# Storing a mixer's split weights one use later, another order of places for them, and one state update moved by a unit

## The chip, the cores and the metric

The kernel runs on one core of one Trainium2 chip. The metric is the time of one execution on the device, in microseconds (us); a comparison uses the median of several executions. A core has five engines that run at the same time and meet through semaphores: TensorE (PE in the profile; PEld is its weight load), VectorE (DVE), ScalarE (ACT), GpSimd (POOL) and SyncE (SP), which here only issues DMA transfers. DMA transfers are also issued by ScalarE. Each engine takes its instructions in order.

## The reference

The reference is one step of a decoder layer, for a prompt of 2048 tokens with 16 meta tokens ahead of it, and for 8 samples of 4 tokens with their own states. All is float32, with a model width of 1024.

```
h = rmsnorm(x, norm_mix)
proj = h @ w_in                                  # 1024 -> 2568
lru_x, lru_gate, z, xbc, dt = split(proj)        # 512, 512, 512, 1024, 8
lru_out = rmsnorm(rg_lru(conv(lru_x)) * gelu(lru_gate))
xs, B, C = silu(conv(xbc))
y, state = ssd_chunked(xs, softplus(dt + bias), A, B, C, state)   # chunks of 128 tokens
ssd_out = rmsnorm((y + xs * d) * silu(z))
x = x + concat(lru_out, ssd_out) @ w_out
h = rmsnorm(x, norm_ffn)
g, v = conv(h @ w_up)                            # 1024 -> 2 * 3072
y = rmsnorm(x + (gelu(g) * v) @ w_down, norm_final)
```

`conv` is a short causal convolution over the tokens, `rg_lru` a gated linear recurrence. In `ssd_chunked` each chunk of 128 tokens gives an output within the chunk, an output from the state that came in, and an update of the state: `state = state * decay + B^T (decayed x dt)`. The next chunk's second output needs that state.

## The kernel before

**Precision.** TensorE multiplies in a rounded float32 (float32r). To keep float32's accuracy every operand is split into a high part, `hi = round(x)`, and a low part, `lo = x - hi`, and a product is three matmuls: hi*hi, hi*lo and lo*hi. A raw weight tile of 128 x 1024 (0.5 MB) is loaded by SP into a buffer `wraw`, of which there are two. ScalarE writes `whi` and VectorE `wlo` (lines 109 and 110, `divide`; the first tile's `wlo` is GpSimd's). The pair `whi`/`wlo` has three buffers each, called place `w` below.

**Stages.** Phase A is the mixer, in six row groups (`PLAN_A`): the samples and meta tokens with two prompt tiles (304 columns), four groups of three tiles of 128 tokens (384 columns) and one of two (256 columns). I call them stages 0 to 5. A stage has a main list, written out in `phase_a_tile`. With the dt product among them, it has 20 input projections, each with one weight tile of `w_in`: eight `xbc` tiles, four `lru`, four gate and four `z`. Then come the output projections: for two halves of the columns, two parts (lru and ssd) and each row tile, a unit of twelve matmuls. Each half and part uses two tiles of `w_out`, so eight tiles per stage; these are loaded raw and split in every stage.

Between the main units stand side tasks, in places written by hand (`SLOTS`): the decays (`R`, `decays`, `seg`), a chunk's work in three steps (`chunk2`, `chunk3`, `chunk4`), the recurrence's gates and scan, and the normalising (`norm`) and transposing (`turn`) of the next stage's rows. Stage 0 uses the list `first`, stages 1 to 3 `mid`, stage 4 `mid2`, and stage 5 `last`. `chunk41` is step 4 of the second row tile: two products give the state's update (line 741, into the psum tag `yy`), VectorE adds it to the state `S` (line 742), TensorE transposes `yt` (line 745, tag `tr`) and VectorE adds it to `ys` (line 747). `yt` comes from step 3 (line 728). Each psum tag has two banks. `chunk22` is step 2 of the third row tile: it transposes `xbc` into two banks of `tr` (lines 655, 658 and 660), from which VectorE and ScalarE make that chunk's operands (lines 662 to 668).

**Kept weights.** The 20 tiles of `w_in` are needed in all six stages. Class `Kept` (from line 129) keeps their split parts in DRAM, `khi` and `klo`. At the first use, in stage 0, the tile is loaded raw, split and used, and both parts are stored from its `whi`/`wlo` on ScalarE's DMA queue; `store` (line 160) issues a tile's two stores when the next tile is split. At each later use both parts are loaded by SP (line 151), 1 MB together, with no split. The place of a loaded pair comes from a cycle over five letters:

```
rooms = itertools.cycle("wwwxr")
```

`w` is a pair `whi`/`wlo`, `x` a fourth pair `xhi`/`xlo` in the pool `pa`, and `r` are the two raw buffers `wraw`, which then hold a high and a low part. So five pairs take turns, and since a stage has 20 tiles, a tile has the same place in each stage: positions 4, 9, 14 and 19 are `r`.

**Order.** TensorE's instructions run in the order of the program. For the other engines, from the end of the first norms until the last few units, a planner sets each engine's order at build time: it takes instructions as they become ready in its own timing model, the earlier in the program first. In the loop at the end of `build`, a source is loaded up to two units ahead of its use, four for `Kept`, and split up to two units ahead. A loaded `Kept` tile may only be issued once all raw tiles ahead of it are split.

Phase B, the channel mixer, follows from line 937 on. It uses `wraw`, `whi` and `wlo` in its own way and no `Kept` tile of the mixer.

Of the kernel before, what the change touches and what calls it, by code (L numbers as in the profile page):

```python
# [8 lines left out]
F32 = mybir.dt.float32  # L9
F32R = mybir.dt.float32r  # L10
# [7 lines left out]
P = 128  # L18
# [28 lines left out]
    },  # L47
    "mid": {
# [4 lines left out]
    },  # L53
# [20 lines left out]
def build(tc, i, o):  # L74
# [5 lines left out]
    with contextlib.ExitStack() as es:  # L80
        es.enter_context(tc.manual_schedule(engines={mybir.EngineType.PE}))
        cp = es.enter_context(tc.tile_pool(name="const", bufs=1))
        wp = es.enter_context(tc.tile_pool(name="w", bufs=3))
        pp = es.enter_context(tc.tile_pool(name="ps", bufs=2, space=PSUM))
        hp = es.enter_context(tc.tile_pool(name="h", bufs=1))
        dp = es.enter_context(tc.tile_pool(name="scr", bufs=1, space=DRAM))
        xr = es.enter_context(tc.tile_pool(name="xr", bufs=1, side="right"))
        side = es.enter_context(contextlib.ExitStack())
        pa = side.enter_context(tc.tile_pool(name="pa", bufs=1, side="right"))
# [18 lines left out]
        def divide(hi, lo, raw, E=V):  # L108
            A.activation(hi, raw, AF.Copy)  # L109
            E.tensor_tensor(lo, raw, hi.bitcast(F32), op=SUB)  # L110

        class Plain:
# [5 lines left out]
            def load(self):  # L118
                self.raw = self.room()
                ld(self.raw, self.src)  # L120

            def split(self, E=V):
                hi, lo = (wp.tile([P, 1024], F32R, name=nm, tag=nm) for nm in ("whi", "wlo"))
                divide(hi, lo, self.raw, E)
                self.out = hi, lo, self.raw

        kept, late = {}, []

        class Kept:

            rooms = itertools.cycle("wwwxr")

            def __init__(self, key, src):
                self.key, self.plain = key, Plain(src)
                self.ahead = KEPT_AHEAD

            def load(self):
                if self.key not in kept:
                    kept[self.key] = [dp.tile([P, 1024], F32, name=f"{nm}_{self.key}", tag=f"{nm}_{self.key}")
                                      for nm in ("khi", "klo")]  # L140
                    self.plain.load()
                    return
                room = next(self.rooms)
                if room == "w":
                    parts = [wp.tile([P, 1024], F32R, name=nm, tag=nm) for nm in ("whi", "wlo")]
                elif room == "x":
                    parts = [pa.tile([P, 1024], F32R, name=nm, tag=nm) for nm in ("xhi", "xlo")]
                else:
                    parts = [wp.tile([P, 1024], F32, name="wraw", tag="wraw", bufs=2).bitcast(F32R) for z in range(2)]
                for part, src in zip(parts, kept[self.key]):  # L150
                    ld(part.bitcast(F32), src)
                self.out = (*parts, None)

            def split(self, E=V):
                self.plain.split(E)
                self.out = self.plain.out
                store()
                late.extend((z, part.bitcast(F32)) for z, part in zip(kept[self.key], self.out))

        def store():  # L160

            for dst, src in late:
                A.dma_start(dst, src)
            late.clear()
# [80 lines left out]
        class Halves:  # L245
# [8 lines left out]
            def norm(self, q):  # L254
                rows, load = self.tiles[q]
                x = self.x[q] = k.spare_row() if q == 3 else row_tile()
                y = load(x)
                r = rstd_of(sum_squares(y[:rows], rows, D), rows, D)
                V.scalar_tensor_tensor(x[:rows], y[:rows], r[:rows], gain[:rows], op0=MUL, op1=MUL)
# [71 lines left out]

        flat = [s if hasattr(s, "load") else Plain(s) for fn, srcs in prog for s in srcs]
        loaded, split, used = 0, 0, 0
        early = sum(len(srcs) for _, srcs in prog[:k.begin_b]) + 2
        begin = contextlib.ExitStack()
# [1113 lines left out]
```

## Time and profile before

| | |
|---|---|
| median of 3 runs | 2574.25 us (2573.41 to 2576.53) |
| profiled execution | 2577.11 us, span of its instructions 2575.2 us |
| TensorE busy, share of span | 2461.2 us, 96% |
| VectorE, ScalarE, GpSimd busy | 1828.7, 1123.5, 665.8 us |
| mean granted TensorE clock | 0.982 |
| DMA | 559.80 MB, mean 217 GB/s |
| phase A | to about 956 us of the span |

In a row of the groups or the time line, `wlo<-wraw,whi` names what is written and read, L110 the line of the kernel, and the number in square brackets the idle time of the engine before the instruction and what ended it. A row of the waits has the waiting instruction, what it waited for, the total in us, how often, and the longest. The granted clock is the share of TensorE's full speed that it was given. SPq and ACTq are the queues that issue DMAs, and a DMA's last number is the time from issue to landing. Busy shares of engines that are not the bound say little by themselves: where TensorE is the bound, its idle time and what ended it count.

### The profile page before, as it was taken

The page shows a single profiled execution, that of the slowest core. Times are in us where ns is not written, and L with a number is a line of the kernel's source. Part 1 is how long each engine was busy: PE and PEld are TensorE (multiplying, and loading weights), DVE is VectorE, ACT ScalarE, POOL GpSimd, SP SyncE. Part 2 cuts the span into 40 slices and gives each one's busy share as a digit, 9 for nine tenths or more (in the row PEclk, how much of TensorE's full clock was granted, in tenths as well). Part 3 has the DMA queues.
Part 4 walks back from the last instruction along what each step waited for, and adds up shares of the span by engine and source line. Part 5 has one row for each costly group of instructions (what it writes and reads, how often), then busy time and mean ns, then how long its engine had stood idle before and what let it go on. Part 6 is the DMA issues. An engine that isn't in the chain of part 4 may idle for free.

```text
span 2575.2 us, 42314 instructions
## 1 busy us (share of the span) xinstructions
PE 2461.2 (96%) x15834; PEld 2233.6 (87%) x15834; DVE 1828.7 (71%) x2928; ACT 1123.5 (44%) x1905; POOL 665.8 (26%) x1059
## 2 busy tenths in 40 slices
PE   7889999998999998999998999999999999999998
PEld 6678879798897878988897899998999998999997
DVE  6675767667675767767767777777877777876776
ACT  4443534435353445444545443434443434433333
POOL 3432313223131326544555201101201102100001
PEclk9899999999999999999999999999999999999999
DMA  8657375473744767544646776665876665866663
GB/s 328 216 188 265 111 249 194 137 259 111 263 171 164 271 198 258 201 180 180 222 172 251 269 255 228 226 224 208 296 249 224 221 217 189 306 221 213 213 222 124
DMA packets 173959, 559.80 MB, mean 217 GB/s; under 512 B 25574, under 2 KB 25958, under 8 KB 173756
## 3 DMA queue, kind: packets, MB, share of 16 engines
q1 hardware_dynamic: 163284, 527.60, 58.2%
q10 hardware_dynamic: 10472, 29.50, 3.0%
q8 instruction: 125, 2.05, 0.3%
q14 instruction: 78, 0.64, 0.1%
HBM read 465.70 MB, written 91.34 MB: 216 GB/s over the span
## 4 chain that ended last, share of the span: by engine, by line
PE 66%; DVE 9%; issue 8%; POOL 7%; DMA 5%; ACT 5%; SPq 0%; POOLq 0%; ACTq 0%; DVEq 0%
PE mm L168 28%; PE sg L1172 14%; PE tr L168 9%; PE yy L168 9%; DVE wlo L110 2%; POOL wraw L1014 1%; ACT ws L109 1%; ACT whi L109 1%; POOL wraw L1013 1%; POOL o_fc L1157 1%; DVE cv L545 1%; POOL x L1015 1%; DMA wraw<-in_w_up 1%; DMA wk<-ws 1%; DVE xi L790 1%
## 5 line engine op out<-in xcount | busy, mean ns | idle before, releaser
L1172 PE MATMUL sg<-whi,ph 128*128 128x512 f32 x1320 | 424.1, 394 | 5.5 <-DVE acc L1176 5.5
L110 DVE TENSOR_TENSOR wlo<-wraw,whi 128x1024 fp32r<-128x1024 f32 x258 | 321.6, 1248 | 130.2 <-ACT whi L109 127.5
L109 ACT ACTIVATE whi<-wraw 128x1024 fp32r<-128x1024 f32 x259 | 272.9, 1056 | 243.2 <-PE sg L1172 90.1
L168 PE MATMUL mm<-hhi,whi 128*128 128x384 f32 (+4 forms) x1024 | 326.5, 319 | 7.7 <-ACT xr L536 6.5
L168 PE MATMUL mm<-hlo,whi 128*128 128x384 f32 (+4 forms) x1024 | 320.0, 312 | 0.9 <-DVE hlo L243 0.9
L168 PE MATMUL mm<-hhi,wlo 128*128 128x384 f32 (+4 forms) x1024 | 319.8, 312 | 1.1 <-DMA wlo<-klo 1.1
L1161 DVE SCALAR_TENSOR_TENSOR c<-u,fcw,c 128x512 f32<-128x512 f32 (+1 forms) x384 | 298.3, 791 | 23.7 <-ACT c L1159 14.1
L1172 PEld LDWEIGHTS sg<-whi,ph 128*128 128x128 f32 x1320 | 247.9, 188 | 65.0 <-DVE acc L1176 7.7
L1157 POOL COPY o_fc<-u 128x2 f32<-128x2 f32 x192 | 85.4, 445 | 807.2 <-DVE u L1066 696.3
L1172 PE MATMUL sg<-wlo,ph 128*128 128x512 f32 x660 | 258.6, 392 | 0.3 <-DVE wlo L110 0.3
L168 PEld LDWEIGHTS mm<-hhi,whi 128*128 128x128 f32 x1024 | 197.7, 193 | 12.7 <-ACT xr L536 7.0
L1159 ACT ACTIVATE c<-u,fcb,fcw 128x512 f32<-128x512 f32 (+1 forms) x192 | 157.8, 823 | 111.6 <-DVE u L1066 109.0
L168 PEld LDWEIGHTS mm<-hlo,whi 128*128 128x128 f32 x1024 | 197.3, 193 | 2.9 <-DVE hlo L243 1.2
L168 PEld LDWEIGHTS mm<-hhi,wlo 128*128 128x128 f32 x1024 | 197.1, 193 | 1.5 <-DMA wlo<-klo 1.5
L168 PE MATMUL yy<-h,ws 128*128 128x256 f32 x1476 | 196.4, 283 | 0.0
L168 PE MATMUL tr<-h,ws 128*128 128x256 f32 x1440 | 191.3, 282 | 2.0 <-DMA ws<-wk 2.0
L168 PEld LDWEIGHTS yy<-h,ws 128*128 128x128 f32 x1476 | 185.8, 189 | 1.0
L168 PE MATMUL mm<-h,ws 128*128 128x256 f32 x1404 | 185.8, 282 | 0.0
L545 DVE SCALAR_TENSOR_TENSOR cv<-xr,packed,cv 128x384 f32<-128x384 f32 (+2 forms) x216 | 150.6, 697 | 47.3 <-ACT cv L543 43.9
L168 PEld LDWEIGHTS tr<-h,ws 128*128 128x128 f32 x1440 | 180.5, 189 | 2.9 <-issue 2.2
L168 PEld LDWEIGHTS mm<-h,ws 128*128 128x128 f32 x1404 | 175.4, 188 | 0.5
L1172 PEld LDWEIGHTS sg<-wlo,ph 128*128 128x128 f32 x660 | 124.1, 188 | 25.2 <-DVE wlo L110 1.1
(321 smaller groups left out, 5377.5 us busy)
## 6 DMA issues: line engine op xcount, KB each, us to landing
ws<-wk SPq DMA_DIRECT2D x288, 512.0 KB, 4.9
wraw<-in_w_up SPq DMA_DIRECT2D x97, 512.0 KB, 4.9
wk<-ws SPq DMA_DIRECT2D x96, 512.0 KB, 6.4
wraw<-in_w_down SPq DMA_DIRECT2D x94, 512.0 KB, 4.9
wlo<-klo SPq DMA_DIRECT2D x60, 512.0 KB, 5.0
whi<-khi SPq DMA_DIRECT2D x60, 512.0 KB, 3.3
wraw<-in_w_out SPq DMA_DIRECT2D x48, 512.0 KB, 3.7
wraw<-in_w_up SPq DMA_DIRECT2D x72, 256.0 KB, 5.1
```

Of the source, the lines that this page charges most:

```text
L109: A.activation(hi, raw, AF.Copy)
L110: E.tensor_tensor(lo, raw, hi.bitcast(F32), op=SUB)
L168: PE.matmul(ps, l, r, start=(k == 0), stop=(k == len(pairs) - 1))
L545: V.scalar_tensor_tensor(cv[:, 3:W], buf[:, t:t + NC], w[:, t:t + 1], cv[:, 3:W], op0=MUL, op1=ADD)
L790: V.tensor_tensor_scan(h[:, 3:W], a4[:, j, 3:W], m4[:, j, 3:W], hc[:, j:j + 1], op0=MUL, op1=ADD)
L1013: G.tensor_tensor(v1, v0, v1, op=ADD)
L1014: G.tensor_tensor(v0, g0, v0, op=SUB)
L1015: G.tensor_tensor(g0, v1, g0, op=SUB)
L1157: G.tensor_copy(o_fc[:, g, NS, :], u[:, W - 2:W])
L1159: A.activation(cv[:, 2:W], u[:, 2:W], AF.Identity, scale=fcw[:, g, 2:3], bias=c["fcb"][:, g:g + 1])
L1161: V.scalar_tensor_tensor(cv[:, 2:W], u[:, z:z + W - 2], fcw[:, g, z:z + 1], cv[:, 2:W], op0=MUL, op1=ADD)
L1172: PE.matmul(ps, l, r, start=first and n == 0, stop=last and n == len(seq) - 1)
```

## The change

Three things change; what is computed stays the same.

1. A `Kept` tile counts its uses. Stage 0 loads it raw, splits it and stores nothing. Stage 1 loads it raw again and splits it again, now into one of four pairs in the order `wwwx`, and stores both parts (on ScalarE's queue, issued when the next tile is split). Stages 2 to 5 load the parts, as stages 1 to 5 did before. So 20 of 100 loads of pairs become raw loads with a split, and the stores move from stage 0 to stage 1.
2. The places of loaded parts follow `rwwxw`: positions 0, 5, 10 and 15 of a stage are `r`, the last one is `w`.
3. In stages 1 to 3 `chunk41` stands after the next main unit (the last gate projection), directly ahead of `chunk22`.

```diff
     "mid": {
-        12: "chunk40 R2 gates2", 13: "gates3 scan chunk21", 14: "chunk31 lru0", 15: "seg2 norm0 chunk41 lru1",
-        16: "chunk22 norm1 lru2", 17: "lru3 chunk32", 18: "chunk42 ssd0 rstd0 norm2", 19: "ssd1", 20: "ssd2",
+        12: "chunk40 R2 gates2", 13: "gates3 scan chunk21", 14: "chunk31 lru0", 15: "seg2 norm0 lru1",
+        16: "chunk41 chunk22 norm1 lru2", 17: "lru3 chunk32", 18: "chunk42 ssd0 rstd0 norm2", 19: "ssd1", 20: "ssd2",
...
         class Kept:
 
-            rooms = itertools.cycle("wwwxr")
+            rooms = itertools.cycle("rwwxw")
+            spare = itertools.cycle("wwwx")
+            uses = {}
...
             def load(self):
-                if self.key not in kept:
-                    kept[self.key] = [dp.tile([P, 1024], F32, name=f"{nm}_{self.key}", tag=f"{nm}_{self.key}")
-                                      for nm in ("khi", "klo")]
+                self.use = self.uses[self.key] = self.uses.get(self.key, -1) + 1
+                if self.use < 2:
                     self.plain.load()
                     return
                 room = next(self.rooms)
-                if room == "w":
-                    parts = [wp.tile([P, 1024], F32R, name=nm, tag=nm) for nm in ("whi", "wlo")]
-                elif room == "x":
-                    parts = [pa.tile([P, 1024], F32R, name=nm, tag=nm) for nm in ("xhi", "xlo")]
+                if room == "r":
+                    parts = [wp.tile([P, 1024], F32, name="wraw", tag="wraw", bufs=2).bitcast(F32R) for z in range(2)]
                 else:
-                    parts = [wp.tile([P, 1024], F32, name="wraw", tag="wraw", bufs=2).bitcast(F32R) for z in range(2)]
+                    parts = pair(room)
                 for part, src in zip(parts, kept[self.key]):
                     ld(part.bitcast(F32), src)
                 self.out = (*parts, None)
 
             def split(self, E=V):
-                self.plain.split(E)
-                self.out = self.plain.out
+                if self.use == 0:
+                    self.plain.split(E)
+                    self.out = self.plain.out
+                    return
+                parts = kept[self.key] = [dp.tile([P, 1024], F32, name=f"{nm}_{self.key}", tag=f"{nm}_{self.key}")
+                                          for nm in ("khi", "klo")]
+                hi, lo = pair(next(self.spare))
+                divide(hi, lo, self.plain.raw, E)
+                self.out = hi, lo, self.plain.raw
                 store()
-                late.extend((z, part.bitcast(F32)) for z, part in zip(kept[self.key], self.out))
+                late.extend(zip(parts, (hi.bitcast(F32), lo.bitcast(F32))))
+
+        def pair(room):
+            pool = pa if room == "x" else wp
+            return [pool.tile([P, 1024], F32R, name=room + nm, tag=room + nm) for nm in ("hi", "lo")]
```

## The prediction

> **What bounds the kernel now.** I read the page first, then the busy time by stage, then what TensorE waited for, and last the time line around its longest waits. I call the six row groups of the mixer stages 0 to 5. Stage 0 is from 16 us to 208.5 us, stage 1 to 366 us, stage 5 ends at 956 us, and the channel mixer fills the rest.
>
> ```profile
> span 2575.2 us, 42314 instructions
> PE 2461.2 (96%) x15834; PEld 2233.6 (87%) x15834; DVE 1828.7 (71%) x2928; ACT 1123.5 (44%) x1905; POOL 665.8 (26%) x1059
> ...
> L110 DVE TENSOR_TENSOR wlo<-wraw,whi 128x1024 fp32r<-128x1024 f32 x258 | 321.6, 1248 | 130.2 <-ACT whi L109 127.5
> L109 ACT ACTIVATE whi<-wraw 128x1024 fp32r<-128x1024 f32 x259 | 272.9, 1056 | 243.2 <-PE sg L1172 90.1
> ```
>
> ```profile
> 16.00:208.50 192.50, 166.18 (x898) 134.75 (x897) 132.59 (x259) 83.52 (x176) 62.07 (x118) 0.90 0.68 244
> 208.50:366.20 157.70, 150.41 (x832) 135.28 (x831) 107.46 (x178) 67.17 (x119) 43.68 (x62) 0.98 0.54 187
> ```
>
> The columns of the second fence are the stretch, its length, busy time of TensorE, weight load, VectorE, ScalarE and GpSimd with counts, granted clock, DMA share and GB/s. TensorE is the bound. So the change is worth what it takes from TensorE's waits and from its half-rate time. Its largest waits, with how often and the longest:
>
> ```profile
> PE mm L168 <- ACT xr L536: 6.5, 2, 4.3
> PE tr L660 <- DVE xbc L639: 5.4, 2, 4.4
> PE tr L658 <- DVE ys L747: 4.4, 1, 4.4
> PE yy L701 <- DMA sst<-in_st_ss: 2.2, 1, 2.2
> ```
>
> ```profile
> PE mm L168 <- ACT whi L109: 22.9, 5, 4.9
> PE yy L741 <- DVE yt L728: 7.1, 4, 1.8
> PE mm L168 <- DVE wlo L110: 2.7, 5, 0.7
> ```
>
> The first fence is stage 0 (18.5 us in four rows), the second stages 1 to 5 (32.7 us in three). In the second, the two rows on whi and wlo are one event in each stage: the first output projection waits for its weights. In stage 1 it reads so:
>
> ```profile
> 320.64 0.34 PE L168 MATMUL mm<-hhi,wraw 128*128 128x384 f32 x1
> 320.83 6.58 SPq L120 DMA_DIRECT2D wraw<-in_w_out  x3
> ...
> 325.84 0.80 PE L168 MATMUL mm<-whi,yhi 128*128 128x512 f32 x1 [4.86 <-ACT whi L109]
> ```
>
> The last input projection (the fourth z tile) has its weights in the two `wraw` buffers. With the room order `wwwxr` and 20 tiles in a stage, positions 4, 9, 14 and 19 are `r`, so the last one always is. `w_out` is loaded into the same two buffers, so its load is issued at 320.83, when that projection has been read, and the load and the split lie bare. After the wait TensorE runs at half rate:
>
> ```profile
> 325.65:332.48 6.83, 6.16 (x14) 4.49 (x15) 2.67 (x3) 2.25 (x3) 0.33 (x1) 0.50 0.51 156
> 482.66:489.49 6.83, 5.55 (x12) 4.07 (x13) 2.42 (x3) 2.71 (x3) 0.94 (x1) 0.50 0.49 153
> 639.68:646.51 6.83, 4.93 (x11) 3.55 (x12) 2.99 (x3) 3.00 (x5) 1.00 (x1) 0.50 0.50 155
> 796.69:803.52 6.83, 5.93 (x14) 4.26 (x15) 2.47 (x2) 2.41 (x3) 0.55 (x1) 0.50 0.51 154
> 922.98:929.81 6.83, 6.10 (x20) 4.36 (x19) 2.82 (x4) 2.12 (x3) 0.00 (x0) 0.50 0.48 154
> ```
>
> TensorE's busy time in these five windows is 28.7 us at clock 0.50; half of it, 14.3 us, is lost.
>
> **Part 1, the order of places.** `rwwxw` puts `r` on positions 0, 5, 10 and 15. Position 15 is the last gate tile, four units before the end of the projections. Behind it come the four z units, at 4.2 us for a projection (the row of 48 matmuls below, two of them), so both `wraw` buffers come free over 16 us before the first output projection, against a landing of 3.7 us, 1.06 us on ScalarE and 1.25 us on VectorE. The split goes into the `w` pairs of positions 16 and 17, read early too.
>
> ```profile
> 312.54 8.46 PE mm L168 x48
> ...
> 339.01 5.60 PE mm L168 x24
> ```
>
> ```profile
> wraw<-in_w_out SPq DMA_DIRECT2D x7, 512.0 KB, 3.7
> ```
>
> The first fence is the chain of waits of stage 1 (start, length), the second the DMA issues from 316 to 346 us, with the landing time last. Stages 2 to 5 use this order. Stage 1 does not load parts any more, but its last raw tiles leave `wraw` when they are split, some units ahead of use, so the same wait goes there. Removed: 22.9 + 2.7 + 14.3 = 39.9 us, of which 8.4 us in stage 1 (4.86 + 0.48 + 3.08). I leave 1 us in for a residue of the wlo kind: -39 us.
>
> What is late next: position 0 now needs both `wraw` buffers at a stage's end. They are free once the last two `w_out` tiles are split, the later one at the start of the last quarter of the output part. Between that and the first projection lie three output units in a stage of three row tiles (2.8 us each, the row of 24 matmuls above is two), with transposes and the 16 small dt products, about 11 us. The split's 2.3 us and a landing at a stage's end fit:
>
> ```profile
> whi<-khi SPq DMA_DIRECT2D x3, 512.0 KB, 6.0
> ```
>
> That is the DMA view of 496 to 525 us. Positions 1, 2 and 4 use `w` buffers that come free in the same order as before. I cost this at 0; without that cover it is the same 5 us of wait and 3 us of half rate, moved to the other end.
>
> [...]
>
> **Part 2, no stores in stage 0.** 40 stores of 0.5 MB (parts of 20 tiles) leave it. What they cost now:
>
> ```profile
> DMA packets 2791, 10.18 MB, mean 392 GB/s; under 512 B 310, under 2 KB 310, under 8 KB 2788
> q10 hardware_dynamic: 1517, 5.54, 52.3%
> ...
> wraw<-in_w_in SPq DMA_DIRECT2D x4, 512.0 KB, 6.6
> ```
>
> ```profile
> wraw<-in_w_in SPq DMA_DIRECT2D x3, 512.0 KB, 3.5
> ```
>
> The first fence is the DMA view of 30 to 56 us, the second that of 125 to 152 us. In the early stretch the DMA engines are full (q1 and q10 together 100%), over half of it stores, and a raw load lands in 6.6 us instead of 3.5. With two raw buffers a tile's period there is half of landing, whi, wlo and about 0.7 us of handing on: (6.6 + 1.06 + 1.25 + 0.7) / 2 = 4.8 us. At 3.5 us of landing it is 3.3 us, and then VectorE sets it:
>
> ```profile
> L545 DVE SCALAR_TENSOR_TENSOR cv<-xr,packed,cv 128x328 f32<-128x328 f32 x21 | 13.3, 631 | 1.8 <-ACT cv L543 1.4
> ...
> L639 DVE SCALAR_TENSOR_TENSOR xbc<-th,cv 128x272 f32<-128x272 f32 x6 | 2.6, 434 | 0.0
> ...
> L638 DVE SCALAR_TENSOR_TENSOR xbc<-th,cv 128x32 f32<-128x32 f32 x6 | 1.2, 196 | 2.2 <-ACT th L635 2.2
> ```
>
> Three convolution steps of 0.63, 0.43 + 0.20 for `xbc` and wlo's 1.25 make 3.8 us a unit. Gain: 4.8 - 3.8 = 1.0 us x 7 units = 7 us, which contains the 4.3 us wait on xr (L536) and its half rate. I add 1 us for the later waits: **-8 us**. Bounds: 0, if VectorE and the sample-state work set this stage's end anyway; -20, if all four rows of stage 0's waits but the `ys` one go (6.5 + 5.4 + 2.2 = 14.1 us) with some 6 us of half rate.
>
> **Part 3, split and store in stage 1.** There 40 part loads on SP's queue become 20 raw loads, and 20 whi copies (21.1 us of ScalarE), 20 wlo subtractions (25.0 us of VectorE) and the 40 stores, on ScalarE's queue, come in. ScalarE rises from 67 to 88 us of 158, which is hidden. VectorE rises from 107.5 to 132.5 us. Bytes for a projection rise from 1.05 to 1.57 MB; over a unit of about 4.5 us (4.2 and what stands between) that is 350 GB/s, under the 392 of the row above, so raw loads should land in about 6 us: a period of (6 + 3.0) / 2 = 4.5 us, as long as the unit, and the loads start two units ahead. The fourth pair (`x`) gives a store time to land. Each lo store waits on ScalarE's queue for its wlo, with the psum copies behind it; it is issued one split later, when wlo is done.
>
> ```profile
> 208.50:312.00 103.50, 101.55 (x606) 94.56 (x604) 74.77 (x133) 47.49 (x89) 34.74 (x49) 1.00 0.52 183
> 285.20:304.80 19.60, 17.65 (x108) 16.37 (x108) 19.37 (x32) 9.75 (x20) 7.22 (x8) 1.00 0.28 104
> ```
>
> VectorE has 28.7 us idle before 312 us, enough for the splits of all 20 tiles (25 us), but in the stretch of the scan it is busy 19.37 of 19.60 us, and the four pairs allow being ahead by about two tiles, so some two splits must still fall into it: 2.5 us. The nearest case with splits beside the scan is stage 0, where TensorE lost the 4.4 us on `ys` (L747). I take 2.5 us and a little over half of that wait with half rate behind it: **+6 us**. Bounds: 0, and +20, about what stage 0 loses to waits that end at ScalarE and VectorE (6.5 + 5.4 + 4.4) with some half rate.
>
> **Part 4, the state update one unit later** (stages 1 to 3). `chunk41` leaves the place where its first product waits for `yt` (L741, 1.8 us a stage). It now stands right ahead of `chunk22`, whose second psum takes the bank that `chunk41`'s transposes have just filled, so it waits for VectorE's `ys` addition (L747). VectorE is full there (the row above: 0.23 us idle in 19.60), and `chunk32` needs VectorE's decay products from the end of that stretch. So TensorE's wait moves: I take 0. Bounds per stage: -1.8 (all of it), and +2.6 (the 4.4 us of stage 0 on the same addition less 1.8).
>
> **Sum** against this execution's 2577.1 us (span 2575.2): -39 - 8 + 6 + 0 = -41, so 2536 us; the median is 2.9 us lower, 2574.25, so **2533 us**.
>
> **Rivals.**
> - *Stage 1 pays more.* VectorE with 132.5 us of work in a stage of 150 us cannot follow, and several waits come with half rate: +20 instead of +6. For it: the full 19.6 us stretch. Against: the 28.7 us idle before. 2547 us.
> - *The change does not free `w_out`.* ScalarE's order puts the whi copy of the first `w_out` tile late, or position 0 waits in turn. The five waits stay or move to the next stage's start; parts 2 and 3 remain: -2, so 2572 us. Against it: at 320.83 the load goes out 0.2 us after the matmul that ends the buffer's use, so the buffer was the cause.
> - *Slower.* Stage 1 becomes bound by raw loads: loads and stores share full DMA engines as in 30 to 56 us, in 20 units. Against a gain of 47 us elsewhere, the period must rise from about 4.5 to over 6.9 us in all 20 units, a landing of about 11 us. At 12 us the period is 7.5, the loss 3.0 x 20 = 60 us, against 47 gained: 2574 + 13 = 2587 us. Against it: the full queue of 30 to 56 us gave 6.6 us.
>
> **How the numbers follow.** The forecast gets 0.67, stage 1 paying more 0.18, `w_out` not freed 0.09, slower 0.06. The forecast's own bounds are 2533 - 12 (part 2) - 6 (part 3) - 5 (part 4), that is 2510, to 2533 + 8 + 14 + 8, or 2563. All four ends do not meet, so for 8 in 10 I take 2514 to 2556, which holds the first rival. A measurement here tells 0.2% (5 us) from no change. Faster by more: forecast, first rival and most of what lies between it and the second, 0.89; the same: 0.05, from the second; slower: 0.06.
>
> **What would show it.** Right: in stages 2 to 5 `w_out` is issued during the z units, and the first output projection follows the last z matmul with under 1 us of wait at clock 1.00; stage 0's raw loads land in about 3.5 to 4 us and it ends near 200 us; stage 1 shows new waits on VectorE rows between the gates and the z tiles. Wrong: the whi wait still there, a wait on `wraw<-khi` at a stage's first projection, raw loads of stage 1 that land in over 8 us, or a different channel mixer, on which I count no change.

## The result, and the profile after

The changed kernel takes 2539.23 us (median of 4 runs, 2534.04 to 2540.29) against 2573.83 us for the kernel before, timed beside it (4 runs, 2572.99 to 2576.53). The ratio is 0.986 with a 95% interval of 0.9843 to 0.9877, so it is faster by 1.2 to 1.6%. The profiled execution took 2538.72 us. On its page the span and the busy times read:

```profile
span 2536.6 us, 42313 instructions
PE 2447.7 (96%) x15834; PEld 2229.1 (88%) x15834; DVE 1854.5 (73%) x2948; ACT 1140.4 (45%) x1925; POOL 691.2 (27%) x1059
```

TensorE has the same 15834 matmuls and is still 96% busy. It has 13.5 us less busy time, although its work is the same: less of it ran at half rate (mean granted clock 0.988, before 0.982). By stage, before (stages 0 and 1) and after (stages 0 to 5), with the columns that the prediction explained (stretch, length, TensorE, weight load, VectorE, ScalarE, GpSimd, clock, DMA share, GB/s):

```profile
16.00:208.60 192.60, 166.28 (x899) 134.78 (x898) 132.59 (x259) 83.62 (x176) 62.07 (x118) 0.90 0.68 244
208.60:366.20 157.60, 150.31 (x832) 135.25 (x831) 107.46 (x178) 67.07 (x119) 43.68 (x62) 0.98 0.54 187
```

```profile
16.00:181.60 165.60, 153.88 (x898) 127.52 (x897) 135.30 (x260) 85.53 (x177) 72.86 (x118) 0.97 0.46 154
181.60:349.40 167.80, 154.50 (x832) 138.08 (x831) 130.12 (x197) 83.64 (x137) 52.47 (x62) 0.96 0.71 244
349.40:501.40 152.00, 148.33 (x831) 134.99 (x830) 107.55 (x178) 67.54 (x119) 44.53 (x62) 0.99 0.56 197
...
653.30:803.50 150.20, 146.95 (x823) 132.50 (x822) 104.85 (x175) 65.01 (x115) 43.63 (x60) 1.00 0.56 199
803.50:917.80 114.30, 107.24 (x753) 97.14 (x752) 86.96 (x165) 58.52 (x121) 35.04 (x58) 0.97 0.74 241
```

Stage 0 is shorter by 27.0 us, stage 1 longer by 10.2, stages 2 to 5 shorter by 5.6, 5.1, 5.6 and 3.9, and the channel mixer by 1.6. That is 38.6 us, the whole difference of the two spans. The forecast of 41 us was near, but two stages moved otherwise than its sum had them: stage 0 gained three times as much as it was given, and stage 1 lost where it was to gain.

What TensorE waited for (total, times, longest) in stage 1, and in stages 2 and 3 together:

```profile
PE mm L178 <- ACT xr L550: 5.8, 3, 3.1
PE sg L775 <- DVE cv L555: 4.3, 1, 4.3
```

```profile
PE tr L668 <- DVE ys L757: 7.3, 2, 3.7
```

The waits of 4.0 to 4.9 us on `whi` of `w_out` are gone in every stage, which was the forecast's largest term; what is left before output projections is 1.7 us on `wlo` in stage 1 and 0.8 us or less in the others. In stage 1 three waits on `xr` (ScalarE's copy of a projection out of psum) and one on the convolution `cv` have come in, and in stages 2 and 3 one wait of 3.7 us each on `ys`. In stage 2 the first two loads of `w_out` and the last products read (SP's queue, with the time from the start of the first to the end of the last, then the chain of waits):

```profile
450.47 6.57 SPq L120 DMA_DIRECT2D wraw<-in_w_out  x2
```

```profile
456.37 16.84 PE mm L178 x84
```

The two loads are issued at 450.47 and 456.71 us, in the second of the four z products and at the start of the third. One unbroken piece of 84 matmuls holds the last two z products (48) and the first three output units (36).

### The profile page after: what moved, and what is told of

Same layout as the page of the kernel before. It is cut to its first block, busy times and chain, and to the rows that moved or that the text cites. A ratio compares the mean times of both kernels' runs of the same rounds, so it can differ in the third digit from the quotient of the medians.

```text
span 2536.6 us, 42313 instructions
## 1 busy us (share of the span) xinstructions
PE 2447.7 (96%) x15834; PEld 2229.1 (88%) x15834; DVE 1854.5 (73%) x2948; ACT 1140.4 (45%) x1925; POOL 691.2 (27%) x1059
## 4 chain that ended last, share of the span: by engine, by line
PE 78%; DVE 10%; DMA 3%; ACT 3%; issue 3%; POOL 2%; SPq 0%; DVEq 0%; POOLq 0%; ACTq 0%
PE mm L178 32%; PE sg L1182 16%; PE yy L178 13%; PE tr L178 9%; DVE wlo L110 2%; PE tr L1182 2%; DVE cv L555 1%; DMA wraw<-in_w_up 1%; ACT whi L109 1%; DVE c L1171 1%; DVE xi L800 1%; PE yy L725 1%; PE tr L248 1%; DVE ws L110 1%; PE sg L775 1%
## 5 line engine op out<-in xcount | busy, mean ns | idle before, releaser
L110 DVE TENSOR_TENSOR wlo<-wraw,whi 128x1024 fp32r<-128x1024 f32 x273 | 343.2, 1259 | 137.3 <-ACT whi L109 137.2
L109 ACT ACTIVATE whi<-wraw 128x1024 fp32r<-128x1024 f32 x274 | 288.7, 1056 | 250.3 <-PE sg L1182 90.5
L178 PE MATMUL mm<-hhi,whi 128*128 128x384 f32 (+4 forms) x1048 | 334.9, 320 | 3.5 <-ACT xr L550 3.1
L178 PE MATMUL mm<-hlo,whi 128*128 128x384 f32 (+4 forms) x1048 | 328.1, 313 | 0.9 <-DVE hlo L253 0.9
L178 PE MATMUL mm<-hhi,wlo 128*128 128x384 f32 (+4 forms) x1048 | 328.0, 313 | 0.0
L1171 DVE SCALAR_TENSOR_TENSOR c<-u,fcw,c 128x512 f32<-128x512 f32 (+1 forms) x384 | 298.4, 791 | 23.1 <-ACT c L1169 13.8
```

Of the source, the lines that this page charges most:

```text
L178: PE.matmul(ps, l, r, start=(k == 0), stop=(k == len(pairs) - 1))
L1171: V.scalar_tensor_tensor(cv[:, 2:W], u[:, z:z + W - 2], fcw[:, g, z:z + 1], cv[:, 2:W], op0=MUL, op1=ADD)
```

## The experiments

All stage lengths in one table, in us, by the windows of one profile of each kernel; the rows behind them are shown where a verdict rests on them. Lengths that no edit touches differ between the profiles too: stage 0 is 4.7 us shorter in the kernel with only `chunk41` moved than before.

| kernel | time | stage 0 | 1 | 2 | 3 | 4 | 5 |
|---|---|---|---|---|---|---|---|
| before | 2573.8 | 192.6 | 157.6 | 157.6 | 157.0 | 155.8 | 118.2 |
| after | 2539.2 | 165.6 | 167.8 | 152.0 | 151.9 | 150.2 | 114.3 |
| order alone | 2538.3 | 192.4 | 149.4 | 149.4 | 149.4 | 148.6 | 112.0 |
| `chunk41` alone | 2585.8 | 187.9 | 160.7 | 160.6 | 160.6 | 156.1 | 119.8 |
| after, `chunk41` back | 2531.3 | 166.0 | 167.4 | 149.6 | 149.4 | 149.7 | 111.8 |
| after, order back | 2568.9 | 165.7 | 167.4 | 161.8 | 160.6 | 158.0 | 120.5 |

### The order of places

The first kernel is the one before with only the order changed, the second the changed kernel with only the order put back.

```diff
-            rooms = itertools.cycle("wwwxr")
+            rooms = itertools.cycle("rwwxw")
```

> The kernel before with the order of places rwwxw and nothing else. Theory: the wait of the first output projection on whi and the half rate behind it go in stages 1 to 5, 36 to 39 us, stage 0 stays at 192.6 us: 2536 to 2538 us, stages 1 to 4 near 149.5 us, stage 5 near 111. Rival, that the order frees w_out no earlier or that position 0 then waits: 2570 us or more.

> The changed kernel with the order of places wwwxr. Theory: the whi waits of 4 to 5 us and their half rate come back in stages 2 to 5 and not in stage 1, which loads no parts: about 30 us more than the changed kernel, near 2569 us. Rival, that something else than the place of the last tile freed w_out: 2539 us.

With the order alone the time is 2538.26 us, ratio 0.9853 (0.9824 to 0.9883): as fast as the whole change. Its stage 1:

```profile
208.40:357.80 149.40, 147.36 (x832) 133.39 (x831) 108.65 (x178) 67.44 (x119) 44.55 (x62) 1.00 0.57 198
```

The clock is 1.00, and TensorE is idle for 2.0 us in the stage. In the waits of stages 1 to 5 no row on `whi` is left; the largest is the one on `yt`, 7.1 us as before. Stages 1 to 5 together take 708.8 us instead of 746.3, so Part 1 is worth 37.5 us of span, against 39 forecast. With the order put back the time is 2568.93 us (one run), 29.7 us above the changed kernel's, and the waits of stages 1 to 5 read:

```profile
PE mm L178 <- ACT whi L109: 17.7, 4, 4.9
```

Four of the five `whi` waits are back. So the rival that the change does not free `w_out` is out. And since the order alone gives the whole gain, the rest of the change must come to about nothing in sum.

### `chunk41` one unit later

Both kernels differ by one line of the slots: the kernel before with the change's line, and the changed kernel with the old line.

```diff
-        ... 15: "seg2 norm0 chunk41 lru1", 16: "chunk22 norm1 lru2",
+        ... 15: "seg2 norm0 lru1", 16: "chunk41 chunk22 norm1 lru2",
```

> The kernel before with chunk41 moved in stages 1 to 3 and nothing else. From the changed kernel's stages 2 and 3 (a new wait of 3.7 us on ys, with half rate behind it, for the 1.8 us on yt): about +3.5 us in each of three stages, 2584 us. The prediction's zero: 2574 us. Rival, that the move gains its wait: 2569 us.

> The changed kernel with chunk41 back in its old place. Theory: the 3.7 us waits on ys and their half rate go from stages 2 and 3 and the 1.0 us from stage 1, the 1.8 us on yt come back: 7 to 9 us less than the changed kernel, 2531 us. Rival, that the move pays or is neutral: 2539 us or more.

Alone, the move makes the kernel slower: ratio 1.0037 (1.0023 to 1.0052). Its stage 1 is 160.7 us long instead of 157.6, and its waits in stages 1 to 3 are:

```profile
203.90:364.60 160.70, 151.58 (x831) 137.00 (x830) 107.90 (x178) 67.88 (x119) 43.58 (x62) 0.97 0.53 184
```

```profile
PE mm L168 <- ACT whi L109: 14.6, 3, 4.9
PE tr L658 <- DVE ys L747: 11.0, 3, 3.7
```

In each stage a wait of 3.7 us on `ys` has taken the place of the 1.8 us on `yt`. The same wait in stage 2 of the changed kernel, in the time line, and the two windows of half rate of stages 2 and 3:

```profile
441.63 0.44 PE L668 MATMUL tr<-ident,xbc 128*128 128x128 f32 x2 [3.67 <-DVE ys L757]
```

```profile
442.98:446.39 3.41, 3.41 (x13) 3.41 (x12) 3.41 (x6) 1.41 (x3) 1.79 (x2) 0.50 0.00 0
593.16:596.57 3.41, 2.86 (x11) 2.87 (x12) 2.92 (x6) 0.96 (x3) 1.04 (x1) 0.50 0.02 5
```

The wait is 1.9 us longer than the one that it replaces, and 3.41 us of half rate follow, in which TensorE was busy for 3.41 and 2.86 us at clock 0.50; half of that, 1.4 to 1.7 us, is lost by my estimate. Together that is 3.3 to 3.6 us; by the table the move made stage 2 of the changed kernel longer by 2.4 us, and by the row above stage 1 of the kernel before by 3.1. In the changed kernel with the old line, the wait of 1.8 us on `yt` brought no window of half rate with it in stages 2 and 3, which run at clock 1.00 (stage 2, and the waits of both):

```profile
349.40:499.00 149.60, 147.50 (x831) 133.25 (x830) 108.67 (x178) 67.54 (x119) 44.72 (x62) 1.00 0.57 201
```

```profile
PE yy L751 <- DVE yt L738: 3.5, 2, 1.8
```

That kernel takes 2531.31 us, ratio 0.9829 (0.9803 to 0.9856). It was run again on another chip:

> The kernel chunk_back once more, on the chip of late_first, as its base: 2531 us.

There it took 2534.20 us, ratio 0.9846 (0.9833 to 0.9859). It is 5 to 8 us below the changed kernel by the medians. The intervals of its two ratios overlap with that of the changed kernel (0.9843 to 0.9877), so the times alone do not settle it. The stages do: with the order `rwwxw`, stages 2 and 3 take 150.8 to 153.2 us in the four kernels of this document with the new line, and 149.3 to 150.1 us in the six with the old one. In those two stages the change is better without its line of `chunk41`.

### What the stores cost in stage 0

Stage 0 got 27 us shorter. To see whether it is the stores, the changed kernel stores its parts in stage 0 as well, into tensors of their own that nothing reads. The second kernel issues the same 40 stores, but of 32 bytes per partition.

```diff
                     self.plain.split(E)
                     self.out = self.plain.out
+                    store()
+                    for nm, part in zip(("ehi", "elo"), self.out):
+                        extra = dp.tile([P, 1024], F32, name=f"{nm}_{self.key}", tag=f"{nm}_{self.key}")
+                        late.append((extra, part.bitcast(F32)))
```

```diff
-                        late.append((extra, part.bitcast(F32)))
+                        late.append((extra[:, 0:8], part[:, 0:8].bitcast(F32)))
```

> The changed kernel with its 40 stores of stage 1 and, in stage 0, 40 more stores of the split parts (to DRAM that nobody reads) at the places where the kernel before had them. If the stores were what stage 0 lost time to: stage 0 back from 165.6 to about 190 us, the other stages as in the changed kernel, about 2563 us. If stage 0's gain came from elsewhere (the places, the planner's order): near 2539 us.

> The same with the 40 extra stores cut to 32 bytes of each partition: as many issues on ScalarE's queue with the same waits, hardly any bytes. Theory, the DMA engines are full: stage 0 stays near 166 us, 2540 us. Rival, the issues and their waits on ScalarE's queue cost the time: stage 0 near 190 us, 2563 us.

Stage 0 with the full stores, and with the small ones:

```profile
16.00:205.90 189.90, 164.75 (x900) 134.19 (x899) 134.01 (x260) 84.85 (x177) 61.83 (x119) 0.91 0.67 240
```

```profile
16.00:185.10 169.10, 151.97 (x899) 125.44 (x898) 137.10 (x260) 85.63 (x177) 71.53 (x119) 0.97 0.47 151
```

With the full stores it takes 189.9 us, 24.3 more than without, and the whole kernel 2558.22 us. With as many small ones it takes 169.1 us, 3.5 more. So it is mainly their bytes, and not their place on ScalarE's queue (one run each). In the same stretch as in the prediction, 30 to 56 us, the changed kernel's DMA view now has

```profile
wraw<-in_w_in SPq DMA_DIRECT2D x6, 512.0 KB, 3.5
```

so raw loads land in 3.5 us instead of 6.6, as forecast. Where in stage 0 the time was won is seen by cutting it at the last transpose of `chunk20`, which starts at 70.56 us before and at 64.53 us after. The two pieces before, then the two after:

```profile
16.00:70.56 54.56, 41.79 (x265) 39.05 (x263) 40.68 (x104) 23.14 (x55) 17.79 (x42) 0.93 0.93 350
70.56:208.60 138.04, 124.49 (x635) 95.73 (x636) 91.90 (x155) 60.48 (x122) 44.29 (x78) 0.89 0.58 202
```

```profile
16.00:64.53 48.53, 42.32 (x264) 39.73 (x262) 42.00 (x108) 28.58 (x71) 25.54 (x47) 0.93 0.51 169
64.53:181.60 117.07, 111.56 (x634) 87.79 (x635) 93.30 (x153) 56.95 (x107) 47.32 (x72) 0.99 0.44 147
```

The first piece, in which the raw loads had been late, is 6.0 us shorter, and that is idle time of TensorE, not busy time. The second piece is 21.0 us shorter: 12.9 us less busy time for the same matmuls, and 8.0 us less idle time. The busy time is half rate that is gone; before, five windows of 30.7 us in all stood in the second piece (the first of them from just ahead of the cut), of which these are the first two:

```profile
69.65:76.48 6.83, 5.92 (x24) 5.83 (x25) 4.48 (x11) 2.99 (x11) 1.02 (x6) 0.50 0.79 297
93.54:103.78 10.24, 10.24 (x23) 4.91 (x23) 3.39 (x5) 2.30 (x4) 3.77 (x7) 0.50 0.69 225
```

After, one window of 3.41 us is left there. Of the waits of this piece, 2.2 us on a load of the states (`sst<-in_st_ss`) and 2.1 us on `xo` are gone, and the 4.4 us on `ys` are 3.1. By which path the stores lengthened each of them was not tested.

### What stage 1 pays for

In the next kernel the parts are stored in stage 0, as before the change, and stage 1 loads and splits raw tiles but stores nothing.

```diff
                 if self.use == 0:
                     ...
+                    store()
+                    late.extend((z, part.bitcast(F32)) for z, part in zip(parts, self.out))
                     return
...
                 store()
-                late.extend(zip(parts, (hi.bitcast(F32), lo.bitcast(F32))))
...
```

> The changed kernel with the parts stored in stage 0, as before, while stage 1 still loads raw tiles and splits them into four pairs but stores nothing. Stage 0 near 192 us. Theory, stage 1 pays for the splits (VectorE, and GpSimd beside it): stage 1 stays at 164 to 168 us, total about 2565 us. Rival, stage 1 pays for the stores' bytes: stage 1 near 152 us, total about 2550 us.

Stage 1 (2559.32 us in all, one run), the raw loads from 210 to 270 us, near its beginning, and the same row of the changed kernel for 182 to 245 us:

```profile
205.90:371.90 166.00, 154.11 (x832) 138.47 (x831) 130.85 (x197) 83.95 (x137) 53.73 (x62) 0.96 0.39 127
```

```profile
wraw<-in_w_in SPq DMA_DIRECT2D x14, 512.0 KB, 3.5
```

```profile
wraw<-in_w_in SPq DMA_DIRECT2D x12, 512.0 KB, 5.2
```

Stage 1 is about as long without stores (166.0 us at 127 GB/s) as with them (167.8 us at 244 GB/s), though raw loads land in 3.5 us instead of 5.2. So the rival of a stage bound by raw loads is out, and to leave out the stores does not make the stage short. That they cost nothing does not follow: the end of this section shows where the time goes in each kernel. Two kernels change who does the split, both with `chunk41` in its old place. In the first, every other low part of stage 1 is made on GpSimd; in the second, ScalarE writes the low parts as copies of the raw tile and leaves the subtraction out.

```diff
-                divide(hi, lo, self.plain.raw, E)
+                divide(hi, lo, self.plain.raw, G if self.key % 2 else E)
```

```diff
-                divide(hi, lo, self.plain.raw, E)
+                A.activation(hi, self.plain.raw, AF.Copy)
+                A.activation(lo, self.plain.raw, AF.Copy)
```

> chunk_back with the low parts of every other tile of stage 1 computed by GpSimd instead of VectorE. If VectorE's amount of work is what stage 1 lacks: 12.5 us of it go, stage 1 falls from 167 to about 160 us, 2524 us. Rival, VectorE is slowed whenever GpSimd works beside it (its convolution steps of 0.62 us took 2.1 to 2.3 us at places), or the 3.4 us of a GpSimd subtraction come too late: stage 1 at 167 us or more, 2531 us or more.

> chunk_back with stage 1's 20 subtractions on VectorE left out: ScalarE writes the low part as a second copy of the raw tile (1.05 us each), so the values of all stages from 1 on are wrong, and only the time of stage 1 is looked at. Theory, stage 1 pays 18 us for 25 us more on VectorE: without them stage 1 falls from 167 to 150 to 154 us, in spite of 21 us more on ScalarE. Rival, what it pays for is the raw load, the copy on ScalarE's queue or the stores: stage 1 stays at 164 us or more.

Stage 1 with GpSimd's help, and with the copies:

```profile
182.10:359.50 177.40, 156.51 (x832) 138.52 (x831) 134.96 (x187) 82.96 (x137) 73.88 (x72) 0.95 0.67 231
```

```profile
183.50:349.40 165.90, 153.92 (x832) 138.48 (x831) 111.37 (x179) 100.85 (x158) 45.90 (x64) 0.96 0.70 248
```

The first is 10.0 us longer than the 167.4 of the kernel that it was made from (2542.53 us in all, one run). The second has 19 us less of VectorE's work than the changed kernel and 17 us more of ScalarE's, and the stage is 1.5 us shorter than 167.4 (2528.0 us in all, one run). So to take this work from VectorE and give it to ScalarE does not make the stage short either. The last kernel asks whether the splits of some tiles cost more than those of others. It also keeps `chunk41` in its old place, stores the parts of positions 8 to 19 in stage 0 and loads them as parts in stage 1; only the 8 tiles of the `xbc` units are split twice.

```diff
-                if self.use < 2:
+                self.place = (self.key - 12) % 20
+                self.raw_uses = 2 if self.place < 8 else 1
+                if self.use < self.raw_uses:
...
-                room = next(self.rooms)
+                room = "wwwrxwwrwxww"[self.place - 8] if self.use == 1 else "rwwxw"[self.place % 5]
...
```

> The changed kernel with chunk41 in its old place, and the 12 tiles from the lru tiles on (positions 8 to 19 of a stage) stored at their first use and loaded as parts in stage 1; only the 8 xbc tiles are loaded raw and split twice. If stage 1 pays for its splits by their number (18 us for 20), 8 of them cost about 7 us and 24 stores in the part of stage 0 where the DMA engines are not full cost under 5 us: stage 0 at 166 to 171 us, stage 1 at 155 to 158 us, 7 us less than chunk_back, about 2524 us. Rival, that the splits among the xbc tiles alone carry the cost, or that stores cost stage 0 wherever they stand: stage 1 near 167 us or stage 0 near 180 us, 2531 us or more.

Stages 0 and 1:

```profile
16.00:195.80 179.80, 160.94 (x898) 130.94 (x897) 132.51 (x260) 86.03 (x177) 70.23 (x118) 0.91 0.61 210
195.80:355.40 159.60, 151.75 (x831) 136.20 (x830) 117.41 (x185) 72.49 (x125) 47.98 (x62) 0.98 0.63 219
```

The 8 splits make stage 1 10.2 us longer than the 149.4 us of the order alone, out of 18.0 for all 20, and the 24 stores left in stage 0 make that stage 13.8 us longer than 166.0. The time, 2531.18 us, ratio 0.9836 (0.9823 to 0.9849), cannot be told from the two results without these edits, 2531.31 and 2534.20 us.

Where in stage 1 the time goes is seen by cutting the stage at the same instruction in each kernel: the first product of the gates (`sg<-cv`), which stands behind ten of the twenty projections, all eight `xbc` units among them. The lengths in us:

| kernel | first ten units | rest of stage 1 |
|---|---|---|
| order alone | 47.0 | 102.4 |
| after | 61.0 | 106.8 |
| after, `chunk41` back | 60.1 | 107.3 |
| after, stage 1 without stores | 53.5 | 112.5 |
| `chunk41` back, half of the low parts by GpSimd | 64.3 | 113.1 |
| `chunk41` back, low parts copied by ScalarE | 54.7 | 111.2 |
| `chunk41` back, only `xbc` tiles split twice | 57.1 | 102.5 |

The rows of the first ten units, with the order alone, after the change, without stores and with ScalarE's copies:

```profile
208.40:255.40 47.00, 47.00 (x273) 45.36 (x272) 31.12 (x59) 17.13 (x33) 12.54 (x24) 1.00 0.76 269
181.60:242.60 61.00, 51.00 (x273) 47.92 (x271) 43.39 (x70) 26.77 (x44) 15.41 (x21) 0.94 0.81 286
205.90:259.40 53.50, 49.24 (x274) 46.65 (x272) 45.38 (x72) 28.73 (x46) 19.71 (x23) 0.97 0.46 148
183.50:238.20 54.70, 49.00 (x273) 46.80 (x271) 30.75 (x58) 35.29 (x53) 11.90 (x21) 0.96 0.83 308
```

With the order alone TensorE does not stop for 47.0 us. After the change the same matmuls take 61.0 us: TensorE is idle for 10.0 us and runs at 0.94, although VectorE is busy for only 71% of that stretch. So it is the order of work between engines that is late, not a full engine. These 14.0 us are most of the 18.4 that stage 1 is longer than with the order alone, and where only the `xbc` tiles are split twice they are all of it (10.1 us).

The stage's length hides what the two experiments did here. With stores and split as in the changed kernel the ten units take 60.0 to 61.0 us in six profiles. Without the stores they take 7.5 us less than in the changed kernel, and with copies by ScalarE in place of VectorE's subtractions 5.4 us less than in the kernel that this was made from. So both the stores and VectorE's part of the split delay the `xbc` units. But the rest of the stage then takes 5.7 and 3.9 us more. The largest waits there are, without the stores, 4.4 us on `ys` and 2.6 us on `yt`; with the copies, 3.1 us on `sacc` from GpSimd and 2.4 us on `gq` from ScalarE. Why these come up there was not tested, nor was a kernel without both.

How a unit comes to be late, the trace suggests as follows. ScalarE's time line shows the `tanh` of successive `xbc` units, before and after the change (start, length, in brackets the wait for VectorE's `cv`), and TensorE's time line after the change the waits on `xr`:

```profile
224.06 0.53 ACT L635 ACTIVATE th<-cv 128x384 f32<-128x384 f32 x1 [2.00 <-DVE cv L545]
230.16 0.53 ACT L635 ACTIVATE th<-cv 128x384 f32<-128x384 f32 x1 [3.88 <-DVE cv L545]
```

```profile
197.85 0.52 ACT L645 ACTIVATE th<-cv 128x384 f32<-128x384 f32 x1 [1.09 <-DVE cv L555]
206.82 0.53 ACT L645 ACTIVATE th<-cv 128x384 f32<-128x384 f32 x1 [6.00 <-DVE cv L555]
210.26 0.52 ACT L645 ACTIVATE th<-cv 128x384 f32<-128x384 f32 x1 [2.32 <-DVE cv L555]
```

```profile
211.22 0.69 PE L178 MATMUL mm<-hhi,whi 128*128 128x384 f32 x1 [3.15 <-ACT xr L550]
224.08 0.44 PE L178 MATMUL mm<-hhi,xhi 128*128 128x384 f32 x1 [1.96 <-ACT xr L550]
```

These are the same two units in both kernels, around the first products of `R`. Before, they start 6.1 us apart, and TensorE does not stop. After, the gap is 9.0 us, in which ScalarE stands for 6.0 us in front of `tanh` with a later copy of psum (`xr`) behind it; TensorE's wait of 3.15 us on `xr` ends at 211.22 us, just after the next `tanh`. That `tanh`, waiting for `cv`, holds up `xr`, and `xr` holds up TensorE, is argued from these rows. It fits that the waits on `xr` in the first ten units are 1.4 us in sum where VectorE makes no low parts, and 4.9 in the kernel that this was made from. What sets the length of the whole stage stays open.

## Why the prediction came out as it did

**Part 1, the order: right.** Forecast -39, measured -37.5 us in stages 1 to 5 with the order alone (-35.4 by the medians). Stage 1 gained 8.2 us (157.6 to 149.4) where the working had 8.4. Position 0 did not become late at the stages' starts, as costed: no first projection of a stage waits for its parts. The half rate, 14.3 us by the estimate from its five windows, stands: in stage 1 TensorE's busy time fell by 2.95 us (150.31 to 147.36), where 3.08 were priced.

**Part 2, no stores in stage 0: the mechanism right, the size three times too small.** Forecast -8, bounds 0 to -20, measured -27.0, and -24.3 by the stores put back. The step "Gain: 4.8 - 3.8 = 1.0 us x 7 units = 7 us" held: 6.0 us by the end of `chunk20`. The term that was mis-sized is "I add 1 us for the later waits", which was 21 us. The bound of -20 took 14.1 us of waits and "some 6 us of half rate". In the stage TensorE's idle time fell by 14.6 us, as that bound had it, but its busy time by 12.4, twice what the bound gave to half rate. The page of before had shown it: stage 0 ran at 0.90, and 37.6 us of windows at 0.50 can be listed there. The prediction listed such windows for stages 1 to 5 and not for stage 0.

**Part 3, split and store in stage 1: mis-sized the other way, and in another place.** Forecast +6, bounds 0 to +20, measured +18.0 (167.4 us with `chunk41` in its old place, against 149.4 with the order alone). It is the size of the first rival, but not quite its reason: without VectorE's subtractions the stage still took 165.9 us. The failed step is "VectorE has 28.7 us idle before 312 us, enough for the splits of all 20 tiles (25 us)": VectorE was busy for 71% of the first ten units while TensorE stood for 10.0 us, so idle time in the stretch was no cover; that each unit's chain has to finish in TensorE's 4.2 us is argued. Of the 18.0 us, 13.1 came in the first ten units and not beside the scan. That loads would land in about 6 us was close (5.2 us over the first 63 us of the stage). The prediction gave the stores and loads of this stage no cost; without the stores the first ten units were 7.5 us shorter, though the stage was not.

**Part 4, `chunk41` later: the new wait foreseen, its price not.** Forecast 0, with bounds of -1.8 to +2.6 per stage; measured +3.0 to +3.6 per stage alone, outside them, and +2.4 and +2.5 in stages 2 and 3 of the changed kernel. "So TensorE's wait moves" was right, and the wait on `ys` was named; that it would be as long as the one it replaced was not. It is 3.67 instead of 1.8 us, and 3.41 us of half rate followed it, which the bound of 2.6 did not hold.

**The sum.** By the table, measured from the order alone: -37.5 (Part 1), -27.0 (stage 0), +18.4 (stage 1), +5.1 (stages 2 and 3), +3.9 (stages 4 and 5, which the other parts were not to touch: 2.3 of it stand in stage 5, which took 110.2 to 112.0 us, not 114.3, in the three kernels that change the stores of stages 0 and 1, so this is spread between profiles at least in part) and -1.6 (channel mixer) make -38.7 us, against -41 forecast. The two large errors, -19 in stage 0 and +12 in stage 1, cancelled in part, and the stages behind took most of the rest. So 2.4 us of the 6 by which the time lies above 2533 come from the sum; most of the rest is the 2.9 us between profiled execution and median, which I took off and which the changed kernel's (2538.72 and 2539.23 us) do not show. The largest term was right; that the sum came so near was luck, because the errors in the others cancelled.

## What to carry to other kernels

Price a stall with the clock that follows it: before costing an edit, list the half-rate windows of every stage that it touches. In stage 0 here TensorE's busy time fell by 12.4 us, its idle time by 14.6. Work moved into a stage was not covered by the sum of idle time here (25 us of splits, 28.7 us idle on VectorE, and the stage 18.0 us longer): price it unit by unit. Compare pieces of a stage between the same two instructions: an edit can win in one piece and lose as much in the next. And test the parts of a change one by one: one line of it gave the whole gain here, two moves cancelled, and the stages that one part touched were shorter without it.

## What was not expected of the hardware

- Half rate came in windows of 3.41, 6.83 and 10.24 us in the traces before and after the change (apart from the last one, at the span's end), and not with every wait. The four waits of 1.8 us on `yt` in stages 1 to 4 before the change had none with them; the waits of 3.7 us on `ys` in stages 2 and 3 of the changed kernel had 3.41 us each, and so had the wait of 1.96 us that ended at 224.08 us in its stage 1. That wait stands in the first row here, the half rate in the second:

```profile
221.11:224.53 3.42, 1.46 (x8) 1.15 (x8) 2.51 (x3) 1.40 (x4) 1.30 (x3) 1.00 0.19 75
224.53:227.94 3.41, 3.41 (x12) 3.41 (x12) 2.66 (x4) 2.78 (x5) 0.65 (x1) 0.50 0.38 154
```

  In the second row the matmuls of 128x384 start 0.32 us apart, and from 228.00 us on, at clock 1.00, 0.17 us. What makes the difference between 1.8 and 1.96 us was not tested. The windows of 6.83 us in the prediction hold the end of the wait: in stage 1 before the change it ends at 325.84 us, and TensorE is busy for 2.74 of the window's first 3.41 us and for all of the rest:

```profile
325.65:329.06 3.41, 2.74 (x6) 1.85 (x7) 2.47 (x2) 1.19 (x2) 0.33 (x1) 0.50 0.30 76
329.06:332.48 3.42, 3.42 (x10) 2.65 (x9) 0.20 (x1) 1.06 (x1) 0.00 (x0) 0.50 0.71 236
```

- VectorE's convolution step took longer where GpSimd's `Rlo` stood beside it. In stages 1 to 4 before the change the eight steps with most of their time beside `Rlo` (2.2 us in the median) took 2.14 to 2.25 us each, the 116 with nothing beside them on GpSimd 0.52 to 0.62. GpSimd's and VectorE's time lines of stage 1 of the changed kernel, at the same moment:

```profile
201.65 1.90 POOL L624 TENSOR_TENSOR Rhi<-packed,dh 128x1024 fp32r<-128x1024 f32 x1 [1.68 <-DVE dh L582]
203.51 2.21 POOL L624 TENSOR_TENSOR Rlo<-packed,dl 128x1024 fp32r<-128x1024 f32 x1
```

```profile
201.70 5.08 DVE L555 SCALAR_TENSOR_TENSOR cv<-xr,packed,cv 128x384 f32<-128x384 f32 x3
```

  Three steps take 5.08 us there; the median step of that stretch takes 0.62 us, so three take 1.9. That GpSimd's work is the cause was not tested apart. It fits the kernel in which GpSimd made half of the low parts. From 181 to 250 us, at the start of its stage 1, and then in the same stretch of the changed kernel, the step's row (total, mean ns) is:

```profile
L555 DVE SCALAR_TENSOR_TENSOR cv<-xr,packed,cv 128x384 f32<-128x384 f32 x28 | 27.1, 968 | 5.0 <-ACT cv L553 4.5
```

```profile
L555 DVE SCALAR_TENSOR_TENSOR cv<-xr,packed,cv 128x384 f32<-128x384 f32 x30 | 25.1, 838 | 2.1 <-ACT cv L553 1.6
```

  With GpSimd's help VectorE's own step was slower there by 130 ns in the mean (one profile each).
